# A decoder layer on one core: the up projection with its input stationary and 512 weight columns moving, turned to features by TensorE transposes

## The chip, the cores and the metric

The kernel runs on one core of one Trainium2 chip. The metric is the device time of one execution in microseconds (us); a lower number is better. The time before is the median of three runs.

## What is computed

One layer of a hybrid decoder on 256 tokens of width 2048, in float32. What matters here is its second half, the channel sub-layer; the first half (adaLN modulation, the combined input projection, differential attention, gated linear attention, output projection) runs ahead of it and is only touched through a shared pool of buffers.

```python
D_MODEL = 2048; SEQ = 256; D_FF = 5632; CONV_WIDTH = 3
...
mod = (c_act @ w_ada[l] + b_ada[l])[:, None, :]
sh1, sc1, gt1, sh2, sc2, gt2 = jnp.split(mod, N_MOD, axis=-1)
...
h2 = rms_norm(x, g_ffn_norm[l]) * (1.0 + sc2) + sh2
u, g = jnp.split(h2 @ w_up[l], 2, axis=-1)
act = jax.nn.gelu(causal_dwconv(g, w_conv[l], b_conv[l]), approximate=False) * u
x = x + gt2 * (act @ w_down[l])
return rms_norm(x, g_final)
```

## The kernel before

Matrices are streamed from HBM in units of 512 KB: two k-tiles of 128 rows by 512 columns. For each unit `load_unit` issues one DMA on SP's queue into a slot of the pool `raw`, ScalarE (ACT) rounds it to a high part `wh` and VectorE (DVE) subtracts it to a low part `wl`. Each k-tile then takes three matmuls per output piece: high times high, high times the low part of the input, low times high. TensorE (PE) needs both parts before it can run a unit. There are three slots for `wh` and three for `wl`.

The pool `raw` has `RAW` = 6 slots. It also takes the adaLN matrix (`raw_a`): `load_unit` lets a generator in the background (`bg`, paced by `rate`) load a piece of `w_ada` and accumulate it on DVE (`acc`, L265). Loads of both kinds go out in one order on SP, and each waits until a slot is free. From the up projection on, two more `raw` slots and one more `wh` and `wl` slot come from a tile that is not needed yet (`late`); they go back after the chunk `NCH - 4`.

There are two block forms. `b_block` keeps a 128 x 128 piece of the weights stationary and moves 256 tokens of the transposed input: the result has features on partitions, and a unit takes 24 matmuls of 256 columns (L142). `a_block` keeps a 128 x 128 piece of the transposed input stationary and moves 512 weight columns: the result has tokens on partitions, and a unit takes 12 matmuls of 512 columns (L176). The down projection (`ps_d`) and some blocks of the input projection (`ps_mm`) already use `a_block`.

The up projection has 11 chunks (`NCH`) of 512 features, each with a gate block and an up block, and 16 k-tiles. For the first 7 chunks (`NSP`) the k-tiles come in groups of 4, 4 and 8, because the normalised input `h2T` becomes ready in such groups. In the first two groups (28 blocks of 2 units) ACT copies a finished accumulator to `spill` and later back into a new accumulator. The last group has 14 blocks of 4 units, and the last 4 chunks have 8 blocks of 8 units. After a gate block's last group the width-3 convolution runs over tokens along the free dimension, four times one ACT operation and two DVE operations (L923, L925), and then GELU; after the up block DVE multiplies the two (L929). Both read the accumulator, with features on partitions. `to_tokens` puts four transposes of the residual (`ps_y`) into each of the first 8 chunks.

A scheduler fixes the order of the instructions on each engine ahead of the run; engines execute in that order and wait on semaphores.

Of the kernel before, what the change touches and what calls it, by code (L numbers as in the profile page):

```python
# [7 lines left out]
F32 = mybir.dt.float32  # L8
# [3 lines left out]
AF = mybir.ActivationFunctionType  # L12
# [3 lines left out]
P = 128  # L16
T = 256
NTB = T // P
# [5 lines left out]
D_FF = 5632  # L24
# [22 lines left out]
def tile_decoder_layer(  # L47
# [4 lines left out]
    PSUM = bass.MemoryType.PSUM  # L52
    V, A, G, PE = nc.vector, nc.scalar, nc.gpsimd, nc.tensor
# [4 lines left out]
    stage = ctx.enter_context(tc.tile_pool(name="stage", bufs=1))  # L58
    ktp = ctx.enter_context(tc.tile_pool(name="ktp", bufs=8))

    RAW, WH, WL = 6, 3, 3

    w_ada_v = w_ada[0].rearrange("(kt p) n -> p kt n", p=P)
    w_in_v = w_in[0].rearrange("(kt p) n -> p kt n", p=P)
# [1 line left out]
    w_up_v = w_up[0].rearrange("(kt p) n -> p kt n", p=P)  # L66
# [41 lines left out]
    def load_unit(view, kt, c0):  # L108
        credit[0] += rate[0]
        while credit[0] >= 1.0:  # L110
            credit[0] -= 1.0
            step()
        fcredit[0] = fcredit[0] + frate[0] if fg else 0.0
        while fcredit[0] >= 1.0:
            fcredit[0] -= 1.0
            fstep()
        if setup and next(setup[0], "end") == "end":
            setup.pop(0)
        raw = slot("raw", [P, 2, 512], F32, "raw", RAW)
        nc.sync.dma_start(out=raw, in_=view[:, kt:kt + 2, c0:c0 + 512])  # L120
        h = slot("wh", [P, 2, 512], F32R, "wh", WH)
        l = slot("wl", [P, 2, 512], F32R, "wl", WL)
        A.activation(h, raw, AF.Copy)  # L123
        V.tensor_tensor(l, raw, h, op=ALU.subtract)  # L124
        return h, l

    def b_block(ps, view, c0, kts, xt, first, last, done=None, tail=0):


        units = kts[::2]  # L130
        rest = None
        groups = [[kt] for kt in units[:len(units) - tail]] + ([units[-tail:]] if tail else [])
        for gi, group in enumerate(groups):
            ws = [(kt, *load_unit(view, kt, c0)) for kt in group]
            seq = [(kt, h, l, j, m) for kt, h, l in ws for j in range(2) for m in range(4)]
            if len(group) > 1:
                seq.sort(key=lambda x: x[4] // 2)
            for kt, h, l, j, m in seq:
                k = kt + j
                ms = slice(m * P, (m + 1) * P)  # L140
                for i, (w, xx) in enumerate(((h, 0), (h, 1), (l, 0))):
                    PE.matmul(  # L142
                        ps[:, m * T:(m + 1) * T], w[:, j, ms], xt[k][:, xx, :],
                        start=(first and k == kts[0] and m % 2 == 0 and i == 0),
                        stop=(last and k == kts[-1] and m % 2 == 1 and i == 2),
                        skip_group_check=True,
                    )
                if rest:
                    rest = (rest[0] - 1, rest[1])
                    if rest[0] == 0:  # L150
                        rest[1]()
                        rest = None
                if done and k == kts[-1] and m % 2:
                    done(m - 1)
                    after = done(m)
                    if rest:
                        rest[1]()
                    rest = (4, after) if after else None
            if rest and group is groups[-1]:
                rest[1]()  # L160

    def a_block(ps, view, c0, kts, xt, first, last, done=None, tail=0):


        units = kts[::2]
        groups = [[kt] for kt in units[:len(units) - tail]] + ([units[-tail:]] if tail else [])
        for group in groups:
            ws = [(kt, *load_unit(view, kt, c0)) for kt in group]
            seq = [(kt, h, l, j, tb) for kt, h, l in ws for j in range(2) for tb in range(NTB)]
            if len(group) > 1:  # L170
                seq.sort(key=lambda x: x[4])
            for kt, h, l, j, tb in seq:
                k = kt + j
                tsl = slice(tb * P, (tb + 1) * P)
                for i, (w, xx) in enumerate(((h, 0), (l, 0), (h, 1))):
                    PE.matmul(  # L176
                        ps[:, tb * 512:(tb + 1) * 512], xt[k][:, xx, tsl], w[:, j, :],
                        start=(first and k == kts[0] and i == 0),
                        stop=(last and k == kts[-1] and i == 2),
                        skip_group_check=True,  # L180
                    )
                if done and k == kts[-1]:
                    done(tb)


    ident = const.tile([P, P], F32, name="ident")
# [128 lines left out]
    psm = p1.enter_context(tc.tile_pool(name="psm", bufs=2, space=PSUM))  # L315
# [10 lines left out]
    ps = pss.tile([P, 512], F32, tag="ms", name="ps_cols")  # L326
# [5 lines left out]
    ps = pss.tile([P, 512], F32, tag="ms", name="ps_bcol")  # L332
# [407 lines left out]
    for k in range(0, KT, 2):  # L740
        ps = pss.tile([P, 512], F32, tag="ms", name="ps_xT")
# [5 lines left out]
    for g, kts in enumerate(KG):  # L747
# [10 lines left out]
        def open_block(bi):  # L758
            ps = psm.tile([P, 1024], F32, tag="mm", name="ps_mm")
            if g:  # L760
                A.activation(ps, pj[BLOCKS[bi][0]], AF.Copy)
            return ps
# [24 lines left out]
        for bi in range(2, NK):  # L787
            ps = open_block(bi)
# [4 lines left out]
    for n, c0, tr in LATER:  # L793
# [5 lines left out]
        ps = psm.tile([P, 1024], F32, tag="mm", name="ps_mm")  # L799
# [45 lines left out]
    for j in range(4):  # L845
# [3 lines left out]
        ps = pss.tile([P, 512], F32, tag="ms", name="ps_cv")  # L849
# [10 lines left out]
    h2T = []  # L860
# [14 lines left out]

    actp = ctx.enter_context(tc.tile_pool(name="actp", bufs=1))
    t2 = ctx.enter_context(tc.tile_pool(name="t2", bufs=1))
    psm = ctx.enter_context(tc.tile_pool(name="psm2", bufs=3, space=PSUM))
    pss = ctx.enter_context(tc.tile_pool(name="pss2", bufs=2, space=PSUM))
    psp[0] = pss  # L880

# [9 lines left out]
    def up_block(ch, i, g, kts):  # L891
        ps = psm.tile([P, 1024], F32, tag="mm", name="ps_h")
        if g:
            A.activation(ps, spill[ch][:, i], AF.Copy)
        b_block(ps, w_up_v, (D_FF, 0)[i] + ch * 512, kts, h2T, g == 0, True)
        return ps

    for g, kts in enumerate(UG[:-1]):
        rate[0] = R_SP
# [7 lines left out]
    def to_tokens(k):  # L907

        pt = pss.tile([P, 512], F32, tag="ms", name="ps_y")
        for j in range(2):  # L910
            for tb in range(NTB):
                PE.transpose(pt[:, j * T + tb * P:j * T + (tb + 1) * P], xT[:, k + j, tb * P:(tb + 1) * P], ident)
        A.activation(xT[:, k:k + 2], pt.rearrange("p (a b) -> p a b", b=T), AF.Copy)
# [2 lines left out]
    rate[0] = R_UP  # L916
    for ch in range(NCH):
        first, kts = (len(UG) - 1, UG[-1]) if ch < NSP else (0, list(range(KT)))
        gv = up_block(ch, 0, first, kts).rearrange("p (m t) -> p m t", t=T)
        y = t2.tile([P, 4, T], F32, tag="w4", name="y", bufs=2)  # L920
        for m in range(4):
            f = ch * 4 + m
            A.activation(y[:, m], gv[:, m], AF.Identity, scale=nconv[:, 2, f:f + 1], bias=nconv[:, 3, f:f + 1])  # L923
            for s in (1, 2):
                V.scalar_tensor_tensor(y[:, m, s:T], gv[:, m, 0:T - s], nconv[:, 2 - s, f:f + 1], y[:, m, s:T],  # L925
                                       op0=ALU.mult, op1=ALU.add)
        A.activation(y, y, AF.Gelu)
        uv = up_block(ch, 1, first, kts).rearrange("p (m t) -> p m t", t=T)
        V.tensor_tensor(y, uv, y, op=ALU.mult)  # L929
        if ch < KT // 2:  # L930
            to_tokens(2 * ch)
        if ch == NCH - 4:
            spare.clear()
        a = actp.tile([P, 2, 4, T], F32R, tag=f"act{ch}", name=f"act{ch}")
        A.activation(a[:, 0], y, AF.Copy)
        V.tensor_tensor(a[:, 1], y, a[:, 0], op=ALU.subtract)
        act += [a[:, :, m] for m in range(4)]
# [43 lines left out]
    for nb in range(4):  # L981
        ps = psm.tile([P, 1024], F32, tag="mm", name="ps_d")

        def done(tb, nb=nb, ps=ps):
            xs = xT[:, 4 * nb:4 * nb + 4, tb * P:(tb + 1) * P]
            cs = slice(nb % 2 * 512, (nb % 2 + 1) * 512)
            dx, sq = (t2.tile([P, 4, P], F32, tag="xv", name=t, bufs=2) for t in ("dx", "sq3"))
            V.tensor_tensor(dx, ps[:, tb * 512:(tb + 1) * 512].rearrange("p (a b) -> p a b", b=P),  # L988
                            gt2[nb // 2][:, cs].rearrange("p (a b) -> p a b", b=P), op=ALU.mult)
            V.tensor_tensor(xs, xs, dx, op=ALU.add)  # L990
            A.activation(sq, xs, AF.Square, accum_out=ssq3[:, tb, nb:nb + 1])
            V.tensor_tensor(xs, xs, gfin[nb // 2][:, cs].rearrange("p (a b) -> p a b", b=P), op=ALU.mult)
            if nb == 3:
                finish_tokens(tb)
# [35 lines left out]
```

## Time and profile before

| what | value |
|---|---|
| median of 3 runs | 1301.42 us (1301.13 to 1303.23) |
| the profiled execution's own time | 1301.91 us |
| its span in the trace | 1300.2 us |
| PE busy in matmuls | 1239.3 us, 95% of the span |
| DVE busy, ACT busy | 888.1 us, 702.3 us |
| moved by DMA | 314.57 MB, 242 GB/s on average |

Times in the trace are microseconds from the start of the span. A matmul's own duration is longer than the step from one to the next, because matmuls overlap in the pipeline; what counts is the step. In rows of stretches each engine has its busy time and, in brackets, its instructions, and then follow the granted TensorE clock, the mean busy share of the DMA engines, and GB/s. In rows of waits stand the total in us, how many, and the longest.

### The profile page before, as it was taken

The page shows a single profiled execution, that of the slowest core. Times are in us where ns is not written, and L with a number is a line of the kernel's source. Part 1 is how long each engine was busy: PE and PEld are TensorE (multiplying, and loading weights), DVE is VectorE, ACT ScalarE, POOL GpSimd, SP SyncE. Part 2 cuts the span into 40 slices and gives each one's busy share as a digit, 9 for nine tenths or more (in the row PEclk, how much of TensorE's full clock was granted, in tenths as well). Part 3 has the DMA queues.
Part 4 walks back from the last instruction along what each step waited for, and adds up shares of the span by engine and source line. Part 5 has one row for each costly group of instructions (what it writes and reads, how often), then busy time and mean ns, then how long its engine had stood idle before and what let it go on. Part 6 is the DMA issues. An engine that isn't in the chain of part 4 may idle for free.

```text
span 1300.2 us, 21317 instructions
## 1 busy us (share of the span) xinstructions
PE 1239.3 (95%) x8492; PEld 1145.4 (88%) x8492; DVE 888.1 (68%) x1137; ACT 702.3 (54%) x913; POOL 38.3 (3%) x79
## 2 busy tenths in 40 slices
PE   4799999999999989899999999999999999999996
PEld 3588898888888889799999999999999988888885
DVE  5788888877667666777765777766667554545454
ACT  5377676854544434566776665744444543434343
POOL 3044000000000000000000000000000000000000
PEclk9899999999999989899999999999999999999999
DMA  8999999875477657699897777766677855555562
GB/s 301 321 346 336 353 336 324 266 236 179 146 232 243 196 170 227 231 360 341 294 336 224 228 225 223 235 215 194 203 233 234 274 168 194 193 194 194 181 208 82
DMA packets 159827, 314.57 MB, mean 242 GB/s; under 512 B 12046, under 2 KB 20942, under 8 KB 159727
## 3 DMA queue, kind: packets, MB, share of 16 engines
q1 hardware_dynamic: 155328, 307.28, 72.4%
q10 hardware_dynamic: 4398, 5.93, 1.3%
q8 instruction: 66, 1.08, 0.3%
q14 instruction: 35, 0.28, 0.1%
HBM read 311.07 MB, written 2.10 MB: 241 GB/s over the span
## 4 chain that ended last, share of the span: by engine, by line
PE 82%; DMA 8%; DVE 5%; ACT 2%; issue 2%; DVEq 0%; ACTq 0%
PE ps_h L142 39%; PE ps_d L176 18%; PE ps_mm L142 8%; PE ps_mm L176 6%; DMA raw_a<-in_w_ada_dram 5%; PE ps_o L142 5%; DVE acc L265 2%; DMA raw<-in_w_in_dram 2%; DVE wl L124 1%; PE ps_mod L233 1%; PE ps_s L590 1%; ACT wh L123 1%; PE ps_a L533 1%; DMA xtok<-in_x_dram 1%; DMA dlam<-in_diff_lambda_dram 1%
## 5 line engine op out<-in xcount | busy, mean ns | idle before, releaser
L124 DVE TENSOR_TENSOR wl<-raw,wh 128x1024 fp32r<-128x1024 f32 x339 | 413.9, 1223 | 220.2 <-ACT wh L123 218.9
L123 ACT ACTIVATE wh<-raw 128x1024 fp32r<-128x1024 f32 x339 | 357.6, 1057 | 372.1 <-PE ps_d L176 123.0
L142 PE MATMUL ps_h<-h2T,wh 128*128 128x256 f32 x2304 | 419.2, 284 | 4.7 <-ACT h2T L302 3.5
L142 PEld LDWEIGHTS ps_h<-h2T,wh 128*128 128x128 f32 x2304 | 360.7, 193 | 5.4 <-ACT h2T L302 3.9
L142 PE MATMUL ps_h<-h2T,wl 128*128 128x256 f32 x1152 | 326.7, 284 | 0.0
L265 DVE SCALAR_TENSOR_TENSOR acc<-raw_a,cols,acc 128x1024 f32<-128x1024 f32 (+1 forms) x180 | 216.3, 1202 | 89.5 <-DMA raw_a<-in_w_ada_dram 88.0
L142 PEld LDWEIGHTS ps_h<-h2T,wl 128*128 128x128 f32 x1152 | 221.7, 192 | 0.0
L176 PE MATMUL ps_d<-wh,act 128*128 128x512 f32 x704 | 217.4, 389 | 0.8 <-DVE dx L988 0.8
L176 PEld LDWEIGHTS ps_d<-wh,act 128*128 128x128 f32 x704 | 132.1, 188 | 29.3 <-DVE dx L988 1.2
L142 PE MATMUL ps_mm<-hT,wh 128*128 128x256 f32 x768 | 144.7, 289 | 7.2 <-ACT wh L123 6.3
L176 PE MATMUL ps_d<-wl,act 128*128 128x512 f32 x352 | 137.8, 391 | 0.0
L142 PEld LDWEIGHTS ps_mm<-hT,wh 128*128 128x128 f32 x768 | 122.5, 196 | 10.3 <-ACT wh L123 6.9
L176 PE MATMUL ps_mm<-wh,hT 128*128 128x512 f32 x384 | 123.9, 398 | 6.1 <-ACT wh L123 5.2
L142 PE MATMUL ps_mm<-hT,wl 128*128 128x256 f32 x384 | 110.8, 290 | 1.5 <-DVE wl L124 1.5
L142 PE MATMUL ps_o<-mixT,wh 128*128 128x256 f32 x512 | 97.3, 291 | 4.5 <-ACT mixT L475 2.6
L142 PE MATMUL ps_h<-h2T,late 128*128 128x256 f32 x768 | 97.4, 283 | 0.0
L142 PEld LDWEIGHTS ps_h<-h2T,late 128*128 128x128 f32 x768 | 94.4, 192 | 0.0
L176 PEld LDWEIGHTS ps_mm<-wh,hT 128*128 128x128 f32 x384 | 73.4, 192 | 22.9 <-ACT wh L123 6.2
L142 PEld LDWEIGHTS ps_o<-mixT,wh 128*128 128x128 f32 x512 | 82.2, 197 | 6.6 <-ACT mixT L475 3.2
L176 PE MATMUL ps_mm<-wl,hT 128*128 128x512 f32 x192 | 77.5, 404 | 2.5 <-DVE wl L124 2.5
L176 PEld LDWEIGHTS ps_d<-wl,act 128*128 128x128 f32 x352 | 66.1, 188 | 13.9 <-issue 0.5
L142 PEld LDWEIGHTS ps_mm<-hT,wl 128*128 128x128 f32 x384 | 74.8, 195 | 2.5 <-DVE wl L124 2.0
(247 smaller groups left out, 1125.2 us busy)
## 6 DMA issues: line engine op xcount, KB each, us to landing
raw_a<-in_w_ada_dram SPq DMA_DIRECT2D x162, 512.0 KB, 5.0
raw<-in_w_up_dram SPq DMA_DIRECT2D x143, 512.0 KB, 4.6
raw<-in_w_in_dram SPq DMA_DIRECT2D x96, 512.0 KB, 5.5
raw<-in_w_down_dram SPq DMA_DIRECT2D x88, 512.0 KB, 4.2
late<-in_w_up_dram SPq DMA_DIRECT2D x33, 512.0 KB, 4.8
raw<-in_w_o_dram SPq DMA_DIRECT2D x32, 512.0 KB, 4.7
raw_a<-in_w_ada_dram SPq DMA_DIRECT2D x32, 256.0 KB, 5.4
late<-in_w_ada_dram SPq DMA_DIRECT2D x14, 512.0 KB, 5.2
```

What stands on the lines that cost most here:

```text
L123: A.activation(h, raw, AF.Copy)
L124: V.tensor_tensor(l, raw, h, op=ALU.subtract)
L142: PE.matmul(ps[:, m * T:(m + 1) * T], w[:, j, ms], xt[k][:, xx, :], start=(first and k == kts[0] and m % 2 == 0 and i == 0), stop=(last an ...
L176: PE.matmul(ps[:, tb * 512:(tb + 1) * 512], xt[k][:, xx, tsl], w[:, j, :], start=(first and k == kts[0] and i == 0), stop=(last and k == k ...
L233: PE.matmul(ps[:, i:i + 1], src[:, i * P:(i + 1) * P], col, start=(not began and i == 0), stop=False, skip_group_check=True)
L265: pin(V.scalar_tensor_tensor(acc, raw[:, j], col, acc, op0=ALU.mult, op1=ALU.add))
L533: PE.matmul(pv[:, i, tb], lhs, rhs, start=True, stop=True)
L590: PE.matmul(pv, q[rs, hb * T + tb * P:hb * T + (tb + 1) * P], k[rs, hb * T:hb * T + n], start=False, stop=(tb == 1), skip_group_check=True)
```

## The change

The up projection calls `a_block` in place of `b_block`. A finished block therefore has tokens on partitions. The new `to_features` has ACT copy the accumulator to a tile in SBUF (`tok`, one buffer), lets PE transpose it in eight pieces of 128 x 128 into a PSUM tile (`ps_tr`, one buffer of two banks), and convolution and multiplication read that. The PSUM banks for it come from the accumulators, 2 in place of 3, and the room in SBUF from the pool `raw`, 5 slots in place of 6, for the whole kernel.

```diff
-    RAW, WH, WL = 6, 3, 3
+    RAW, WH, WL = 5, 3, 3
...
-    psm = ctx.enter_context(tc.tile_pool(name="psm2", bufs=3, space=PSUM))
+    psm = ctx.enter_context(tc.tile_pool(name="psm2", bufs=2, space=PSUM))
+    pst = ctx.enter_context(tc.tile_pool(name="pst", bufs=1, space=PSUM))
...
-        b_block(ps, w_up_v, (D_FF, 0)[i] + ch * 512, kts, h2T, g == 0, True)
+        a_block(ps, w_up_v, (D_FF, 0)[i] + ch * 512, kts, h2T, g == 0, True)
         return ps
+
+    def to_features(ps):
+
+        tok = t2.tile([P, NTB, 512], F32, tag="tok", name="tok")
+        A.activation(tok, ps.rearrange("p (a b) -> p a b", b=512), AF.Copy)
+        tr = pst.tile([P, 1024], F32, tag="tr", name="ps_tr")
+        for m in range(4):
+            for tb in range(NTB):
+                PE.transpose(tr[:, m * T + tb * P:m * T + (tb + 1) * P], tok[:, tb, m * P:(m + 1) * P], ident)
+        return tr.rearrange("p (m t) -> p m t", t=T)
...
-        gv = up_block(ch, 0, first, kts).rearrange("p (m t) -> p m t", t=T)
+        gv = to_features(up_block(ch, 0, first, kts))
...
-        uv = up_block(ch, 1, first, kts).rearrange("p (m t) -> p m t", t=T)
+        uv = to_features(up_block(ch, 1, first, kts))
```

On PE, the first place is the up block of chunk 0 in its last group of k-tiles. In the kernel before, its second unit follows the first with matmuls of 256 columns (`ps_h_7339` is its accumulator, `h2T8` and `h2T10` the input, `wh` and `wl` the weights):

```order
L142 MATMUL ps_h_7339<-h2T8_7111,wl_7347 128x256
L142 MATMUL ps_h_7339<-h2T10_7118,wh_7376 128x256 x2
L142 MATMUL ps_h_7339<-h2T10_7118,wl_7377 128x256
L142 MATMUL ps_h_7339<-h2T10_7118,wh_7376 128x256 x2
L142 MATMUL ps_h_7339<-h2T10_7118,wl_7377 128x256
```

In the changed kernel the same block is `ps_h_6629`, and behind its second unit stand the eight transposes of the gate block before it:

```order
L176 MATMUL ps_h_6629<-wh_6654,h2T10_6470 128x512 x2
L176 MATMUL ps_h_6629<-wl_6655,h2T10_6470 128x512
L176 MATMUL ps_h_6629<-wh_6654,h2T10_6470 128x512
L906 MATMUL ps_tr_6606<-ident_70,tok_6604 128x128 x8
L176 MATMUL ps_h_6629<-wh_6672,h2T12_6480 128x512
L176 MATMUL ps_h_6629<-wl_6673,h2T12_6480 128x512
```

Half as many matmuls stand there, each twice as wide, and the transposes stand two units (24 matmuls) behind the end of the block that they turn. Over the 22 blocks they stand between 1.8 and 4.9 units behind it.

On ACT, the second place is the end of that gate block. In the kernel before, the convolution's first operation (`y_7325`) reads the gate block's accumulator `ps_h_7204` there, behind four weight units:

```order
L894 ACTIVATE ps_h_7474<-spill1_5285 128x1024
L123 ACTIVATE wh_7346<-raw_7344 128x1024
L123 ACTIVATE wh_7376<-raw_7374 128x1024
L123 ACTIVATE wh_7406<-raw_7404 128x1024
L123 ACTIVATE late10_5292<-late9_5291 128x1024
L923 ACTIVATE y_7325<-ps_h_7204,nconv_83 128x256
```

In the changed kernel `tok_6604` copies the gate block's accumulator `ps_h_6531`, and the convolution (`y_6615`) reads the transposed tile:

```order
L123 ACTIVATE wh_6672<-raw_6670 128x1024
L902 ACTIVATE tok_6604<-ps_h_6531 128x1024
L123 ACTIVATE late10_5295<-late9_5294 128x1024
L895 ACTIVATE ps_h_6727<-spill1_5288 128x1024
L123 ACTIVATE wh_6730<-late9_5294 128x1024
L123 ACTIVATE wh_6748<-raw_6746 128x1024
L934 ACTIVATE y_6615<-ps_tr_6606,nconv_83 128x256 x2
```

One copy of 128 x 1024 has come in, and the refill of an accumulator from `spill` stands behind that copy, because the same two banks are filled again.

## Rows read from the trace of the kernel before

**Rows 1.** The page's row of the granted TensorE clock, 40 slices.

```profile
PEclk9899999999999989899999999999999999999999
```

**Rows 2.** Chain of work in order of time, up projection: start, us, what.

```profile
528.65 36.34 PE ps_h L142 x286
...
566.67 57.69 PE ps_h L142 x480
...
720.08 0.44 PE ps_y L912 x4
...
907.83 138.23 PE ps_h L142 x1152
```

**Rows 3.** PE's timeline in the down projection: start, us, engine, line, instruction.

```profile
1100.02 0.39 PE L176 MATMUL ps_d<-wl,act 128*128 128x512 f32 x1
...
1111.58 0.39 PE L176 MATMUL ps_d<-wl,act 128*128 128x512 f32 x1
```

**Rows 4.** Busy time by stretch, up projection: PE, PEld, DVE, ACT, POOL, clock, DMA.

```profile
566.00:626.00 60.00, 60.00 (x503) 60.00 (x504) 47.45 (x45) 38.65 (x42) 0.00 (x0) 1.00 0.97 335
...
744.00:767.50 23.50, 23.50 (x198) 23.50 (x198) 18.57 (x22) 14.95 (x19) 0.00 (x0) 1.00 0.72 231
```

**Rows 5.** Waits from 526 to 720 us: who waited for whom.

```profile
ACT wh L123 <- PE ps_h L142: 32.6, 23, 2.7
...
DVE acc L265 <- DMA raw_a<-in_w_ada_dram: 9.7, 8, 2.4
```

**Rows 6.** Costliest groups by line and shape: busy us, mean ns.

```profile
L265 DVE SCALAR_TENSOR_TENSOR acc<-raw_a,cols,acc 128x1024 f32<-128x1024 f32 x153 | 196.1, 1282 | 81.2 <-DMA raw_a<-in_w_ada_dram 80.0 <-ACT acc L263 0.4
...
L894 ACT ACTIVATE ps_h<-spill 128x1024 f32<-128x1024 f32 x28 | 28.5, 1019 | 0.4
L905 ACT ACTIVATE spill<-ps_h 128x1024 f32<-128x1024 f32 x28 | 28.2, 1007 | 0.0
```

**Rows 7.** Chain of work near the start: a run of transposes.

```profile
16.24 3.63 PE ps_xT L744 x16
```

**Rows 8.** Busy time by stretch, first half, columns as in rows 4.

```profile
75.00:100.00 25.00, 23.95 (x149) 21.18 (x148) 23.02 (x29) 17.55 (x20) 14.84 (x27) 1.00 1.01 351
...
425.00:450.00 25.00, 22.62 (x159) 20.21 (x159) 16.96 (x46) 13.03 (x36) 0.00 (x0) 0.95 0.66 204
```

**Rows 9.** Loads in 125 to 175, 275 to 325 and 425 to 475 us: median us to landing.

```profile
raw<-in_w_in_dram SPq DMA_DIRECT2D x16, 512.0 KB, 5.7
...
raw<-in_w_in_dram SPq DMA_DIRECT2D x12, 512.0 KB, 3.6
...
raw_a<-in_w_ada_dram SPq DMA_DIRECT2D x7, 512.0 KB, 4.0
```

**Rows 10.** Waits of SP's queue from 0 to 528 us.

```profile
SPq L240 <- DVE wl L124: 75.1, 47, 6.9
SPq L120 <- DVE wl L124: 69.9, 45, 3.6
SPq L120 <- DVE acc L265: 48.3, 46, 3.8
```

**Rows 11.** SP's timeline in the output projection: adaLN loads.

```profile
410.85 0.37 SPq L240 DMA_DIRECT2D raw_a<-in_w_ada_dram  x1
...
414.10 0.37 SPq L240 DMA_DIRECT2D raw_a<-in_w_ada_dram  x1
```

**Rows 12.** DVE's timeline in the same stretch: the accumulations of such loads.

```profile
411.65 1.28 DVE L265 SCALAR_TENSOR_TENSOR acc<-raw_a,cols,acc 128x1024 f32<-128x1024 f32 x1 [0.82 <-DMA raw_a<-in_w_ada_dram]
...
419.34 1.28 DVE L265 SCALAR_TENSOR_TENSOR acc<-raw_a,cols,acc 128x1024 f32<-128x1024 f32 x1 [1.62 <-DMA raw_a<-in_w_ada_dram]
```

**Rows 13.** Chain of work from 400 to 470 us, in order of time.

```profile
414.10 5.22 DMA raw_a<-in_w_ada_dram
...
445.60 0.70 DVE mixT L476
...
446.35 4.52 PE ps_o L142 x23
```

## The prediction

> **What bounds the kernel now.** I read the clock row first, then the chain of work through the up projection, then the busy time of its stretches, then the waits, and last the loads of the first half, since the change takes a slot away there too.
>
> The granted TensorE clock is at its upper level, 2.4 GHz, in all but a few slices [rows 1], so a cheaper matmul can't be made up for by a clock that rises. The chain runs through PE from 528.65 us to 907.83 + 138.23 = 1046.06 us [rows 2], apart from a few other rows of PE's own. In the middle stretch PE is busy in 60.00 of 60.00 us, in a late one in 23.50 of 23.50 [rows 4]. So the up projection takes as long as PE's instructions take. ACT and DVE have room: 38.65 and 47.45 of 60 us, 14.95 and 18.57 of 23.5 us. The waits say the same: ACT waits for PE for 32.6 us in 526 to 720 us, and DVE waits 9.7 us for loads [rows 5].
>
> DMA differs from stage to stage. In 566 to 626 us its share is 0.97 at 335 GB/s, since the background loads of `w_ada` run there too; in the late stretch it is 0.72 [rows 4]. The most that this kernel holds over 25 us is 351 GB/s at a share of 1.01 [rows 8]. The early spill groups are therefore nearly bound by two things at once.
>
> **Matmuls.** One matmul of 256 columns costs a step of 138.23/1152 = 0.1200 us [rows 2]. One of 512 columns, in the form that the change uses (weights moving), costs (1111.58 - 1100.02)/51 = 0.2267 us; 51 is the count from the first to the last of these rows [rows 3]. A pair of the old costs 0.2400, so each new one saves 0.0133 us. There are 22 blocks of 8 units of 24 matmuls = 4224 old ones, and 2112 new: 506.9 us become 478.8, **-28.2 us**. A unit falls from 2.88 to 2.72 us.
>
> The page "TensorE: Matmul & The Clock Gate" of the Trainium skill (Back-to-back issue gap) gives 262 cycles for 256 columns and 518 for 512, so merging a pair would save 6 cycles, 2.5 ns, and 2112 of them 5.3 us in place of 28.2. By that the sum below would be 22.9 us higher. The two rows here are of this kernel and of the same data type and differ by 13.3 ns, so the measurement decides.
>
> **Transposes.** 22 blocks x 8 = 176. Four of the same shape take 0.44 us in the midst of this projection [rows 2], 0.11 each: **+19.4 us**. The upper bound is a run of 16 at 3.63/16 = 0.227 each [rows 7], +40 us; I take the nearer row, in the same stage.
>
> So PE's own work falls by 8.8 us only. Where it falls matters. The 28 spill blocks (2 units each, no transposes) save 28 x 2 x 0.16 = 9 us. Of the rest, a chunk of the last k-group has 8 units and two sets of transposes: 23.04 us become 21.77 + 1.76, **+0.5 us** each for 7 chunks; a chunk of 16 units saves 0.8 us, for 4 chunks. Nearly the whole gain lies where DMA is nearly full.
>
> **DMA in the spill groups.** The 60 us stretch would shrink to about 60 x 2.72/2.88 = 56.7 us with the same bytes: 335 x 60/56.7 = 354 GB/s, against 351 held elsewhere. That leaves a wait between nothing and the whole 8.9 us; the nearest row is 351, within 1% of what is wanted, so I take a loss on the lower side, **+2.5 us**.
>
> **Copies and new waits.** 22 `tok` copies by ACT, like the spill copies of the same size, 1.007 and 1.019 us [rows 6]. ACT goes from 15 to about 17 of 23.5 us. The copy and the transposes stand one behind the other, with at least 1.8 units = 4.9 us of matmuls between, against about 1 us for the copy; what hides it is those matmuls, and without them each block would cost PE about 1 us, 22 us in all. Two accumulators in place of three: when a block of 2 units ends, its bank must be emptied (1.0 us) and, in the second and third group, filled again (1.0 us) before the next but one block starts, and there is a block of 5.44 us between. Queued behind these on ACT are the `wh` copies, for which PE waits; ACT is ahead of PE [rows 5]. Bounds 0 and 22 us; near the former: **+1 us**.
>
> **One slot fewer in `raw`.** This works in the first half too, which the change doesn't speak of. SP waits there for slots: 75.1, 69.9 and 48.3 us in its three largest groups [rows 10]. So slots set when a load is issued.
>
> At one place I can follow the chain. In the output projection the load issued at 410.85 us would now get the slot of the `w_ada` piece that DVE works on from 411.65 to 412.93 [rows 12], so it issues about 2.1 us later. It lands 4.0 to 4.8 us later [rows 9], is held for 1.28 us by DVE, and only then lets go the load which now issues at 414.10 [rows 11] and which is the chain's own (5.22 us, up to 419.32; DVE starts on it at 419.34) [rows 12, 13]. That load would issue at 418.2 to 419.1 and land at 422.2 to 424.3: 3 to 5 us late. The chain leads on to `mixT` at 445.60 and PE at 446.35 [rows 13], where PE has 2.4 us of idle time in 25 already [rows 8]. I take **+4 us**.
>
> In the saturated stretches before (351 GB/s), a 524 KB load takes 1.49 us of the DMA. Six slots make a cycle of 9.0 us: 5.7 us from issue to landing [rows 9] and 3.3 us in ACT's and DVE's hands. Five slots want a cycle of 7.5 us. Landing takes only 3.6 us where DMA isn't full [rows 9], and 3.6 + 3.3 = 6.9 is below 7.5, so DMA can stay full: lower bound 0. If landing stayed at 5.7, each load would take 9.0/5 = 1.8 us, 20% more over the 125 us from 75 to 200 us: 25 us. The shorter landing is what fewer loads in flight should give: **+2 us**. The up projection itself has the `late` slots, 7 in place of 8.
>
> **Sum.** 1301.9 (the profiled run) - 28.2 + 19.4 + 2.5 + 1 + 4 + 2 = 1302.6. The median of the runs is 0.5 us below the profiled one: **1302 us**. The bound of what can be told from no change is 0.2%, 2.6 us.
>
> **Rivals.**
> - *Gain kept* (faster). The spill groups hold 354 GB/s and the lost slot costs 0 to 3 us, for landing gets shorter wherever there are fewer loads in flight. Then 1301.4 - 8.8 + 0 to 5: 1292 to 1298 us, about 1294. For it: 351 was held elsewhere [rows 8]. Against it: the chain at 410 to 420 us has a load in it.
> - *Lost slot decides* (slower). The first half loses more than 11 us, from there on the time is above 1306: half of the 25 us bound gives 12.5 + 4, so 1301.4 - 8.8 + 2.5 + 1 + 16.5 = 1313 us. For it: the 193 us of SP's waits for slots [rows 10]. Against it: 6.9 is below 7.5 us.
> - *PE waits for copies and transposes.* One `tok`, one `ps_tr`: if ACT gets to the copy later than 4.9 us, PE stands, and so do all matmuls behind. From 0.5 us on for each of 22, 1302 + 11 = 1313 or more. Against it: ACT's free time [rows 4, 5].
> - *A wide matmul saves next to nothing.* Then 1302 + 22.9 or, at a step of 0.24, 28: 1325 to 1330 us. That is the skill's rule above. Rows 2 and 3 speak against it.
> - *Transposes lower the clock, or run at the bound of 0.227 us.* 1302 + 20.6 = 1323 us. The clock row stays at 9 through this projection though there are `ps_y` transposes in it [rows 1]. The same page (Part 4: PE-mode transpose) says that the clock gate doesn't engage for transposes; four in 0.44 us amid full speed matmuls don't show it, and no run of eight is in this trace.
>
> **Chances.** Gain given back, 1298 to 1306: 0.40. Gain kept, 1292 to 1298: 0.26. Lost slot, 1306 to 1315: 0.25. Waits for transposes: 0.05. Narrow saving 0.02, clock 0.02. Faster takes the second and 0.04 of the first (below 1298.8): 0.30. Within 0.2% (1298.8 to 1304.0) the most of the first, 0.28. Slower: the rest, 0.42. The range is 1291 to 1313, which leaves out the last cases and the tail of the slot case; the likeliest alone has 1298 to 1306.
>
> **What the profile after would show.** A step of 0.2267 us in `ps_h` (right) or near 0.24 (wrong); eight `ps_tr` in 0.88 us with no idle time ahead; PE busy without a gap in the late chunks, where a chunk of 8 units goes from 23.5 to about 24.0 us and one of 16 units falls by 0.8 us. In the spill groups DMA at 0.97 or above, and PE waiting for `wh` or `wl`; without such waits the second case holds. The lost slot shows as a later start of the up projection than 528.65 us: about 534.7 by my terms, the same by the second case, over 540 by the third. I am wrong if PE's waits in the up projection exceed some 5 us, or if the first half ends early or unchanged; then the term of the slot was mine to misjudge.

## The result, and the profile after

| what | value |
|---|---|
| changed kernel, median of 4 runs | 1323.85 us (1318.59 to 1328.09) |
| kernel before, median of 4 runs | 1302.33 us (1301.13 to 1304.54) |
| ratio to the kernel before | 1.0157 (1.0119 to 1.0195): 1.6% slower |
| the profiled execution | 1328.09 us, span 1326.4 us: the slowest of the four |
| PE busy, ACT busy | 1246.7 us and 722.4 us (before 1239.3 and 702.3) |

The two traces show first where the time went. This view lists for a tile each kind of instruction with its count, min/median/max ns, and first and last start. In the kernel before:

```profile
L719 PE MATMUL ps_low<-hT,wlow x32: 274/277/283, 191.2 to 209.2; 128*32 128x256 f32 x32
L850 PE MATMUL ps_cv<-ident,cst x4: 233/256/305, 454.9 to 459.3; 44*128 44x44 f32 x4
L142 PE MATMUL ps_h<-h2T,wh x2304: 278/283/581, 526.6 to 1045.7; 128*128 128x256 f32 x192
```

In the changed kernel, the same view:

```profile
L719 PE MATMUL ps_low<-hT,wlow x32: 276/278/282, 212.0 to 230.0; 128*32 128x256 f32 x32
L850 PE MATMUL ps_cv<-ident,cst x4: 232/256/303, 486.0 to 490.2; 44*128 44x44 f32 x4
L176 PE MATMUL ps_h<-wh,h2T x1152: 387/389/796, 560.0 to 1074.5; 128*128 128x512 f32 x192
L176 PE MATMUL ps_d<-wh,act x704: 387/389/504, 1074.8 to 1315.9; 128*128 128x512 f32 x176
```

`ps_low` stands at the end of the input projection's first part, `ps_cv` in the output projection. The delay is 20.8 us at the first, 31.1 at the second, and 33.4 when the up projection begins. The up projection itself takes 514.5 us in place of 519.1, and the eight `ps_g` (3.4 us) now lie in it, which stood behind it before. So all of the loss arises ahead of what the change rewrites, and the rewritten part is faster.

The next rows are of the changed kernel, at the times of [rows 8] and at two places of its up projection (columns as there). It runs later by then, so the same times don't hold quite the same work:

```profile
75.00:100.00 25.00, 23.26 (x164) 22.02 (x163) 20.48 (x27) 16.84 (x21) 11.13 (x19) 0.91 0.94 303
...
425.00:450.00 25.00, 21.73 (x138) 18.91 (x138) 18.14 (x30) 8.72 (x21) 0.00 (x0) 0.86 0.64 214
593.00:653.00 60.00, 60.00 (x272) 49.90 (x273) 48.12 (x45) 40.78 (x45) 0.00 (x0) 1.00 0.98 352
...
965.34:988.00 22.66, 22.66 (x107) 18.85 (x105) 15.64 (x18) 12.27 (x14) 0.00 (x0) 1.00 0.74 235
```

In the first row 303 GB/s stand where 351 stood, and PE is busy for 23.26 us in place of 23.95, at a granted clock of 0.91 in place of 1.00. In the second PE is busy for 21.73 us in place of 22.62, though a little more was moved (214 GB/s, before 204). The last two rows are of the up projection: PE is busy without a gap, at 352 GB/s in the spill groups, and the clock stays at 1.00 in the last one, which begins with eight transposes. The loads of 125 to 175 us, first group of [rows 9], now take:

```profile
raw_a<-in_w_ada_dram SPq DMA_DIRECT2D x15, 512.0 KB, 5.5
raw<-in_w_in_dram SPq DMA_DIRECT2D x14, 512.0 KB, 5.4
```

The last number is the landing, the median time from a load's issue to its arrival. With six slots it was 5.7 us for `raw` [rows 9], and for `raw_a`:

```profile
raw_a<-in_w_ada_dram SPq DMA_DIRECT2D x10, 512.0 KB, 5.9
```

With five slots the landing has hardly shortened. The prediction had let it fall to 3.6. In the up projection the chain of work (as [rows 2]: the work that ended last, followed back through what released each step) gives the two prices:

```profile
965.34 0.87 PE ps_tr L906 x8
966.22 21.78 PE ps_h L176 x96
```

A matmul of 512 columns takes a step of 21.78/96 = 0.2269 us, a transpose 0.87/8 = 0.109 us. A block of 16 k-tiles with its transposes is 22.66 us, where one took 23.04 (192 x 0.1200): a chunk of two gains 0.8 us, as worked out.

### The profile page after: what moved, and what is told of

It is laid out like the page before. It is cut to its first block, busy times and chain, and to the rows that moved or that the text cites. A ratio compares the mean times of both kernels' runs of the same rounds, so it can differ in the third digit from the quotient of the medians.

```text
span 1326.4 us, 17505 instructions
## 1 busy us (share of the span) xinstructions
PE 1246.7 (94%) x6556; PEld 1061.3 (80%) x6556; DVE 888.6 (67%) x1137; ACT 722.4 (54%) x935; POOL 39.6 (3%) x79
## 4 chain that ended last, share of the span: by engine, by line
PE 66%; DMA 18%; DVE 9%; issue 3%; ACT 2%; DVEq 0%; SPq 0%; ACTq 0%
PE ps_h L176 35%; PE ps_d L176 18%; DMA raw_a<-in_w_ada_dram 12%; DMA raw<-in_w_in_dram 4%; PE ps_o L142 4%; DVE acc L265 3%; PE ps_mm L142 3%; DVE wl L124 3%; PE ps_tr L906 1%; PE ps_mm L176 1%; ACT wh L123 1%; PE ps_mod L233 1%; PE ps_s L590 1%; DMA xtok<-in_x_dram 1%; DMA dlam<-in_diff_lambda_dram 0%
## 5 line engine op out<-in xcount | busy, mean ns | idle before, releaser
L124 DVE TENSOR_TENSOR wl<-raw,wh 128x1024 fp32r<-128x1024 f32 x330 | 402.6, 1223 | 224.6 <-ACT wh L123 223.9
L123 ACT ACTIVATE wh<-raw 128x1024 fp32r<-128x1024 f32 x330 | 348.6, 1057 | 349.3 <-PE ps_d L176 120.3
L176 PE MATMUL ps_h<-wh,h2T 128*128 128x512 f32 x1152 | 366.7, 393 | 4.9 <-ACT h2T L302 3.5
L176 PEld LDWEIGHTS ps_h<-wh,h2T 128*128 128x128 f32 x1152 | 216.5, 188 | 51.4 <-ACT h2T L302 3.9
L176 PE MATMUL ps_h<-wl,h2T 128*128 128x512 f32 x576 | 226.5, 393 | 0.0
L142 PE MATMUL ps_mm<-hT,wh 128*128 128x256 f32 x768 | 150.2, 295 | 11.2 <-ACT wh L123 10.0
L142 PEld LDWEIGHTS ps_mm<-hT,wh 128*128 128x128 f32 x768 | 126.8, 202 | 14.7 <-ACT wh L123 11.0
L176 PEld LDWEIGHTS ps_h<-wl,h2T 128*128 128x128 f32 x576 | 108.7, 189 | 22.6 <-DVE gt L970 0.2
L176 PE MATMUL ps_h<-late,h2T 128*128 128x512 f32 x384 | 94.0, 391 | 0.0
L176 PEld LDWEIGHTS ps_h<-late,h2T 128*128 128x128 f32 x384 | 71.8, 188 | 15.0 <-ACT late L123 0.4
```

Of the source, the lines that this page charges most:

```text
L142: PE.matmul(ps[:, m * T:(m + 1) * T], w[:, j, ms], xt[k][:, xx, :], start=(first and k == kts[0] and m % 2 == 0 and i == 0), stop=(last an ...
L176: PE.matmul(ps[:, tb * 512:(tb + 1) * 512], xt[k][:, xx, tsl], w[:, j, :], start=(first and k == kts[0] and i == 0), stop=(last and k == k ...
```

## The experiments

Ratios are to runs of the kernel before on the same chip, with a 95% interval; their medians were 1302.5 to 1303.7 us. Differences in us below are worked out from the ratios or the medians, which agree to within 1.5 us.

| run | what | median us | ratio |
|---|---|---|---|
| e1 | before, 5 slots | 1328.11 | 1.0207 (1.0180 to 1.0233) |
| e2 | before, 4 slots | 1352.85 (one run) | |
| e3 | before, a 7th slot early | 1295.58 | 0.9952 (0.9933 to 0.9971) |
| e4 | change, 6 slots | 1297.90 | 0.9964 (0.9950 to 0.9978) |
| e5 | change, a 6th slot early | 1304.54 | 1.0010 (0.9999 to 1.0020) |
| e6 | change, 6 slots and a 7th early | 1289.97 | 0.9907 (0.9887 to 0.9928) |
| e7 | before with wide matmuls, no transposes | 1276.06 | 0.9794 (0.9778 to 0.9811) |
| e8 | before, 2 accumulators | 1333.38 | 1.0243 (1.0220 to 1.0265) |
| e9 | before, 2 accumulators, copied out | 1304.77 | 1.0002 (0.9987 to 1.0017) |
| e10 | before, 6th slot as a tile of its own | 1311.31 | 1.0056 (1.0035 to 1.0076) |

**Slots alone: e1 and e2.**

```diff
-    RAW, WH, WL = 6, 3, 3
+    RAW, WH, WL = 5, 3, 3
```

That is e1; e2 has 4 there.

> The kernel before with 5 slots in the pool raw in place of 6 and nothing else changed. Theory S (the lost slot is what made the change slow: fewer loads are in flight in the first half, and a load's landing does not shorten enough): the first matmul of the up projection starts near 560 us in place of 526.6 us, ps_low near 212 in place of 191 us, and the time is about 1335 us (1301.4 plus the 33 us by which the changed kernel's up projection starts late). Rival U (the new block form itself, its pools or its order, slows the program): within 5 us of 1301 us.

Measured 1328.11 us, 26 to 27 us above the kernel before and 7 below what was expected. In its trace the up projection starts 25.6 us late:

```profile
L719 PE MATMUL ps_low<-hT,wlow x32: 276/278/282, 206.8 to 224.8; 128*32 128x256 f32 x32
L850 PE MATMUL ps_cv<-ident,cst x4: 232/256/302, 477.0 to 481.1; 44*128 44x44 f32 x4
L142 PE MATMUL ps_h<-h2T,wh x2304: 278/283/582, 552.2 to 1071.8; 128*128 128x256 f32 x192
```

The up projection takes 519.6 us, against 519.1 in the kernel before. The slot alone costs more than the whole slowdown; rival U falls. Up to the up projection, the loads stand in the same order on SP in the kernel before, in e1 and in the changed kernel, so that isn't the cause either. At the start of the up projection e1 is 8 us less late than the changed kernel's trace, whose run was the slowest of its four. One trace's start is only good to a few us: five kernels with six slots in the pool and the same order of loads (before, e4, e7, e8 and e9) start the up projection between 526.1 and 532.4 us.

> The kernel before with 4 slots. Theory S with a landing that grows with the loads in flight (from 1.3 in flight at 3.6 us and 3.75 at 5.7 us: 2.4 us plus 0.88 us for each) and 3.3 us in the hands of ACT and DVE: 0.52 loads per us, 272 GB/s between 75 and 200 us, and ps_low starts near 230 us. Rival, landing unchanged at 5.7 us whatever is in flight: 4 slots in 9.0 us, 233 GB/s, ps_low near 262 us. My own term of the prediction (landing falls to 3.6 us): 4/6.9 loads per us, 304 GB/s, ps_low near 212 us.

Stretches from 75 to 200 us (columns as in [rows 8]), first of the kernel before, then e1, then e2:

```profile
75.00:200.00 125.00, 121.23 (x770) 108.12 (x769) 106.63 (x126) 90.44 (x102) 28.21 (x53) 1.00 1.00 345
```

```profile
75.00:200.00 125.00, 115.21 (x705) 99.79 (x704) 99.45 (x116) 84.63 (x95) 27.93 (x53) 1.00 0.97 316
```

```profile
75.00:200.00 125.00, 104.15 (x589) 88.49 (x590) 87.36 (x99) 75.09 (x82) 22.66 (x53) 0.95 0.88 282
```

The landing there, in e1:

```profile
raw<-in_w_in_dram SPq DMA_DIRECT2D x37, 512.0 KB, 5.5
raw_a<-in_w_ada_dram SPq DMA_DIRECT2D x29, 512.0 KB, 5.3
```

And in e2:

```profile
raw_a<-in_w_ada_dram SPq DMA_DIRECT2D x32, 512.0 KB, 4.7
raw<-in_w_in_dram SPq DMA_DIRECT2D x32, 512.0 KB, 5.3
```

`ps_low` starts at 233.1 us in e2. Expected were 272 GB/s and 230 us from a landing that grows with the loads in flight, 233 GB/s and 262 us from one that never changes, 304 GB/s and 212 us from my own term. The first is nearest, if not exact: a landing near 5.0 us with four slots is still far from 3.6. A slot's cycle is the time from one load's issue into it to the next. Estimated from the rows as slots divided by loads per us (524 KB each), it is 9.1 us with six, 8.3 with five, 7.4 with four. To keep the 345 GB/s, five slots would have had to turn in 7.6 us. Of the 0.8 us between six and five, the landing gives about 0.3; the rest is the time between landing and next issue, which falls from 3.4 to 2.9 us by this estimate. Why that part falls is not shown.

**One slot more: e3.** From the start to the up projection the ring has a seventh slot, from room that the first half leaves free.

```diff
     c1 = p1.enter_context(tc.tile_pool(name="c1", bufs=1))
+    spare.update(raw=[c1.tile([P, 1024], F32, name="raw7")])
```

> The kernel before with a seventh slot up to the up projection, from room that the first half leaves free. Theory S: the stretch from 50 to 200 us is already at the 351 GB/s that this kernel reaches at most, so at most 4 us there; some of the DVE waits for adaLN pieces between 200 and 520 us go: 1293 to 1300 us. Rival (six slots are enough everywhere, and a slot matters only below six): 1301 us.

Measured 0.9952: 6 us faster.

```profile
L720 PE MATMUL ps_low<-hT,wlow x32: 276/277/282, 189.6 to 207.6; 128*32 128x256 f32 x32
L142 PE MATMUL ps_h<-h2T,wh x2304: 278/283/582, 521.2 to 1040.2; 128*128 128x256 f32 x192
```

`ps_low` starts 1.6 us earlier, the up projection 5.4 us, so most of it seems to come from behind the saturated stretch. In that stretch the seventh slot moves no more (345 GB/s before), and the landing is longer:

```profile
75.00:200.00 125.00, 120.09 (x774) 108.15 (x773) 105.90 (x124) 88.10 (x98) 31.11 (x53) 1.00 1.00 346
```

```profile
raw<-in_w_in_dram SPq DMA_DIRECT2D x41, 512.0 KB, 6.4
raw_a<-in_w_ada_dram SPq DMA_DIRECT2D x31, 512.0 KB, 5.9
```

The rival, that a slot matters only below six, expected 1301 us; the time speaks against it, but the order of the loads on SP differs here too, as e5 and e10 will show.

**The change with its slot back: e4.** `tok` is two halves in the two buffers of the tag `xv`, which are used by the norm ahead and by the down projection behind.

```diff
-    RAW, WH, WL = 5, 3, 3
+    RAW, WH, WL = 6, 3, 3
...
-        tok = t2.tile([P, NTB, 512], F32, tag="tok", name="tok")
-        A.activation(tok, ps.rearrange("p (a b) -> p a b", b=512), AF.Copy)
+        tok = [t2.tile([P, 512], F32, tag="xv", name=f"tok{tb}", bufs=2) for tb in range(NTB)]
+        for tb in range(NTB):
+            A.activation(tok[tb], ps[:, tb * 512:(tb + 1) * 512], AF.Copy)
...
```

The eight transposes, in the lines left out, now go half by half.

> The changed kernel with all 6 slots in raw: tok is two halves of 128x512 in the two buffers of the tag xv, which stand free in the up projection. Theory S: the first half is that of the kernel before, and what is left is the up projection's own gain, 8.8 us less 2.5 and 1 us as in the prediction: 1296 us (1292 to 1299). Rival U: 1318 us or more, as the changed kernel.

Measured 0.9964, 4.7 us faster than the kernel before, inside the expected range. With e1's ratio this gives 1.0207 x 0.9964 = 1.017 for the changed kernel, where 1.0157 (1.0119 to 1.0195) was measured: the lost slot and the rewritten part together account for the result. Its up projection:

```profile
L176 PE MATMUL ps_h<-wh,h2T x1152: 387/389/795, 529.6 to 1044.2; 128*128 128x512 f32 x192
```

And busy time by stretch of its spill groups:

```profile
548.00:568.00 20.00, 20.00 (x98) 16.84 (x97) 14.87 (x13) 12.01 (x13) 0.00 (x0) 1.00 1.04 387
...
566.00:626.00 60.00, 60.00 (x276) 49.98 (x276) 47.72 (x49) 39.05 (x44) 0.00 (x0) 1.00 1.00 360
```

PE has no gap, though the loads take 360 GB/s over 60 us. 351 GB/s was not the most that DMA moves: 387 stand here over 20 us. The trace of the kernel before has such rows too, over 20 us and over 25, which I hadn't read, because I had looked at stretches of 25 us in the first half only:

```profile
548.00:568.00 20.00, 20.00 (x170) 20.00 (x169) 14.34 (x13) 11.63 (x12) 0.00 (x0) 1.00 1.04 380
...
550.00:575.00 25.00, 25.00 (x211) 25.00 (x211) 19.03 (x20) 15.34 (x18) 0.00 (x0) 1.00 1.03 370
```

**Where in the program the slot counts: e5 and e10.** e5 is the changed kernel with `RAW` at 5 and the line of e3; e10 is the kernel before with the same two.

> The changed kernel with its own tok and 5 slots in the pool, and a sixth slot only up to the up projection, from room that the first half leaves free. Theory S (the lost slot costs in the first half alone; in the up projection 7 slots do as well as 8): the time of the changed kernel with 6 slots all through, 1297 us (1294 to 1300). Rival T (the up projection's spill groups, near the most that DMA moves, need the eighth slot): some 5 us or more above that, 1302 us or more.

Measured 1304.54 us, 0.1% above the kernel before and 6.6 us above e4, as rival T had it. But the trace shows otherwise:

```profile
L720 PE MATMUL ps_low<-hT,wlow x32: 274/277/282, 197.7 to 216.2; 128*32 128x256 f32 x32
L176 PE MATMUL ps_h<-wh,h2T x1152: 387/389/795, 537.8 to 1051.0; 128*128 128x512 f32 x192
```

The up projection with 7 slots takes 513.2 us, no more than e4's 514.6 with 8; it only starts late, 537.8 us against 529.6. What differs in the first half is the order of the loads on SP. A slot that is a tile of its own makes the scheduler write another order; soon after the start, e4 (-) and e5 (+, where `raw_91` is the sixth slot):

```order
-L120 DMA raw<-in_w_in_dram 128x2x512
-L240 DMA raw_a<-in_w_ada_dram 128x2x512 x2
-L120 DMA raw<-in_w_in_dram 128x2x512
-L240 DMA raw_a<-in_w_ada_dram 128x2x512 x2
-L120 DMA raw<-in_w_in_dram 128x2x512
-L240 DMA raw_a<-in_w_ada_dram 128x2x512 x2
-L120 DMA raw<-in_w_in_dram 128x2x512
+L120 DMA raw_91<-in_w_in_dram 128x2x512
+L240 DMA raw_a<-in_w_ada_dram 128x2x512 x2
+L120 DMA raw<-in_w_in_dram 128x2x512
+L240 DMA raw_a<-in_w_ada_dram 128x2x512
+L120 DMA raw_91<-in_w_in_dram 128x2x512
```

The third load of `w_in` has moved ahead of one of `w_ada`.

> The kernel before with 5 slots in the pool and a sixth, only up to the up projection, as a tile of its own, as in the changed kernel's run with a sixth early slot. Theory O (a slot that is a tile of its own changes the order in which SP's loads are written, and that order costs the 8 us by which the up projection started late there): up projection near 535 us, time near 1309 us. Rival T (it is the up projection that wants the eighth slot): up projection near 527 us and a longer up projection, or no loss at all, 1302 us.

Measured 1.0056, as theory O had it:

```profile
L142 PE MATMUL ps_h<-h2T,wh x2304: 278/283/582, 535.8 to 1055.4; 128*128 128x256 f32 x192
```

The up projection is 9.2 us late, outside the 526.1 to 532.4 us named above, and takes 519.6 us. With six slots in number, the sixth as a tile of its own costs 7 to 9 us, all of it in the first half. That its order of loads does this, and which load, is argued and not shown apart. It also means that the seventh slot's worth in e3 and e6 is not separated from the order that came with it.

**The merged matmuls alone: e7.**

```diff
-        b_block(ps, w_up_v, (D_FF, 0)[i] + ch * 512, kts, h2T, g == 0, True)
+        a_block(ps, w_up_v, (D_FF, 0)[i] + ch * 512, kts, h2T, g == 0, True)
```

> The kernel before (6 slots, 3 accumulators) with the up projection's weights moving, and no copy to tok and no transposes: convolution and product read the accumulator as it lies, so features and tokens are mixed up there. It has the merged matmuls alone. By the prediction's terms (4224 x 0.1200 becomes 2112 x 0.2267 us, DMA keeps up): 28.2 us below the kernel before, 1274 us (1272 to 1278). Rival (loads bind once PE is faster, or a wide matmul saves next to nothing): 1285 us or more.

Measured 0.9794: 26.8 us faster, against 28.2 by the term. This kernel leaves out the copies and the transposes, so it doesn't compute the layer. From e7 to e4 it is 22 us more for copies, transposes and one accumulator fewer, against 19.4 for the transposes by the term.

By the cycles that the page "TensorE: Matmul & The Clock Gate" of the Trainium skill (Back-to-back issue gap) gives for a single matmul by itself, e7 would be only an estimated 5.3 us below the kernel before; the 26.8 us measured decide against that estimate here.

**Two accumulators: e8 and e9.**

```diff
-    psm = ctx.enter_context(tc.tile_pool(name="psm2", bufs=3, space=PSUM))
+    psm = ctx.enter_context(tc.tile_pool(name="psm2", bufs=2, space=PSUM))
```

> The kernel before with 2 accumulators in place of 3 from the up projection on. By the prediction's term (nothing of 22 us): within 2 us of 1302 us. Rival (a bank that is emptied and filled again in time only with three): 1306 us or more.

Measured 1.0243, 31 us slower: my expectation was wrong. From 526 to 720 us, nearly all of it ahead of the first convolution (709.8 us), PE is as busy as in the kernel before (192.65 and 192.14 of 194 us). Behind that PE waits for the refill from `spill`, six times and 16.6 us in all:

```profile
PE ps_h L142 <- ACT ps_h L894: 16.6, 6, 4.3
```

In two stretches PE is idle for 9.1 and 7.3 us, and the granted clock stands at 0.94 and 0.91; in the kernel before PE has no gap there, at 1.00 (busy time by stretch):

```profile
720.00:800.00 80.00, 70.90 (x552) 69.92 (x552) 49.80 (x55) 43.51 (x52) 0.00 (x0) 0.94 0.59 184
800.00:860.00 60.00, 52.71 (x407) 52.30 (x407) 37.83 (x44) 31.31 (x36) 0.00 (x0) 0.91 0.60 189
```

The waits explain about half of the 31 us; by these rows the lower clock bears on the rest, but its price is not measured apart. The chain of work at one such wait:

```profile
720.71 0.89 ACT late L123
721.60 0.08 issue
721.68 1.06 ACT xT L913 x2
722.74 0.02 issue
722.76 1.28 ACT L927
724.04 0.01 issue
724.05 1.06 ACT y L927
725.11 0.93 ACT ps_h L894
726.04 0.04 issue
726.08 1.11 PE ps_h L142 x6
```

PE has nothing to do until `ps_h` is filled again, and the refill stands on ACT behind GELU (`y` L927; the row `L927` ahead of it is a load of ACT's function table). In the old form the convolution and the product read the accumulator itself, so its PSUM banks are free only after them. In e9 ACT copies the finished block first, and both read the copy:

```diff
+        c = [t2.tile([P, 2, T], F32, tag="xv", name=f"copy{i}", bufs=2) for i in range(2)]
+        for i in range(2):
+            A.activation(c[i], ps[:, i * 512:(i + 1) * 512].rearrange("p (m t) -> p m t", t=T), AF.Copy)
+        return [c[m // 2][:, m % 2] for m in range(4)]
...
-        gv = up_block(ch, 0, first, kts).rearrange("p (m t) -> p m t", t=T)
+        gv = copied(up_block(ch, 0, first, kts))
...
```

> The kernel before with 2 accumulators, and ACT copies each finished block of the last k-groups to SBUF (two halves of 128x512), from which convolution and product read. Theory C (with 2 accumulators PE waits until convolution and product have read the old one; a copy frees it after about 1 us): the 31 us of the run with 2 accumulators go, 1302 us (1300 to 1306). Rival (the refill from spill itself is what comes late with 2): 1320 us or more.

Measured 1.0002: the 31 us are gone, and PE's waits on the refill with them. For `ps_h` it now waits only for the input `h2T`, as in the kernel before:

```profile
PE ps_h L142 <- ACT h2T L302: 3.5, 1, 3.5
...
PE ps_h L142 <- DVE h2T L307: 1.3, 1, 1.3
```

So in the kernel before two accumulators cost 31 us without a copy and nothing with one. The copy to `tok` empties an accumulator in the same way, so it is most likely what lets the changed kernel do with two; no run takes it out of the changed kernel.

**Both gains: e6.** e4 with the line of e3.

> The changed kernel with 6 slots all through (tok in the two buffers of xv) and the seventh slot up to the up projection. If the two gains lie in different stages and add (0.48% from the seventh slot, 0.36% from the up projection): 1302 x 0.9952 x 0.9964 = 1291 us (1288 to 1294). Rival (both gains are covered by one later wait): 1296 us.

Measured 1289.97 us, 0.9907: the gains add, and this beats the kernel before by 13 us and the changed one by 34. Its trace, of a run of 1293.51 us, starts the up projection at 527.5 us, so it doesn't show in which stage the gain of the early slot lies.

## Why the prediction was wrong, point by point

**The step that failed** is the slot in the saturated stretches: "+2", between bounds of 0 and 25 us, because "The shorter landing is what fewer loads in flight should give". What happened lies near the bound that I set aside: `ps_low` is 20.8 us late in the changed kernel's trace and 15.6 in e1's. By the start of the up projection it is 33.4 and 25.6 us, against +6 for both terms of the slot in the sum. The working took the two landings of [rows 9], 5.7 us with DMA full and 3.6 where it isn't, as a choice of two, and then needed only 6.9 below 7.5. But 3.6 stands in a stretch (275 to 325 us) where 189 GB/s are moved; in no row read here do such a landing and a full DMA stand together. In the saturated stretch the landing was about 5.7, 5.4 and 5.0 us with six, five and four slots. With one slot fewer the cycle shortened by 0.8 us, where 1.5 were needed, so DMA could not stay full: 316 GB/s in e1 against 345.

**The place at 410 us** had +4. From `ps_low` to the up projection the changed kernel loses another 12.6 us and e1 10.0; up to `ps_cv` it is 10.3 and 6.5. Between `ps_low` and `ps_cv` loads of `w_ada` have 49% of the changed kernel's chain and 30% of e1's, against 14% in the kernel before. So the mechanism was right, but it was followed at one place and acts at several. (The 4.8 us in its working is the landing of the load issued at 410.85 us, not a row of [rows 9].)

**The matmuls** had -28.2 us (506.9 less 478.8 is 28.1); e7 measured 26.8, and the step is 0.2269 us against 0.2267. Right. **The transposes** had +19.4: 176 x 0.109 = 19.2 us, and the nearer row was the right one; the upper bound of 0.227 us and the rival of a lower clock fall by the row of 965 to 988 us above. (The clock row isn't at 9 all through the projection, as the prediction says: the slice in which it starts has 8, well ahead of the first `ps_y`.)

**DMA in the spill groups** had +2.5 and cost nothing: 360 GB/s over 60 us with PE busy all through (e4). The most that I set, 351 GB/s over 25 us, was only the most of the stretches that I had read; 370 stand in the trace of the kernel before.

**Copies and accumulators** had +1. In e4 PE waits for neither; in the changed kernel's trace it waits twice, 1.4 us in all, for a copy to `spill`. The value was right and the reason incomplete: by e8 and e9 two accumulators are harmless in the kernel before only with a copy.

**The chances.** The rival "lost slot decides" had 0.25 and named the mechanism that decided; its time, 1313 us, took half of the bound. The whole of it would have given 1325, close to the 1323.85 measured, but in part by luck: 25 us is more than the saturated stretch lost, 4 us is less than the stretches behind it lost, and of the +2.5 nothing came. The range ended at 1313, though 25 us was a bound of an unknown cost and belonged in it.

## What to carry to other kernels

Before a buffer is taken out of a shared ring, look at the stage where the ring is busiest, whatever stage the edit is meant for: there, slots divided by (landing plus holding) is the rate in loads. Here the landing shortened by less than the slots: from six to four, a third fewer, it fell by an eighth. So don't price a lost slot with the landing of a queue that has little in it. And a copy that frees a scarce buffer early can be worth more than it costs (e9 against e8); count who holds what until when, before and after.

## What the hardware showed that I had not expected

DMA moved 387 GB/s over 20 us and 360 over 60 us, at a busy share of 1.04 and 1.00, beside a PE that had no gap. With five and four slots the busy share in 75 to 200 us was still 0.97 and 0.88, while 316 and 282 GB/s moved in place of 345: the share falls less than the bytes, so here a share near 1 doesn't say that DMA moves all that it can.
